# Moving the second branch's sums and splits into the first block-product units, and giving the output tiles other PSUM banks

## The chip, the cores and the metric

The kernel runs on one core of one Trainium2 chip, as one program with one launch. The metric is the device time of that program in microseconds; the kernel before took 1213.66 us (median of 3 runs, 1212.82 to 1214.16). Five engines take part, each with a queue of its own that it works off in order: TensorE (PE, matrix products into PSUM), VectorE (DVE), ScalarE (ACT), GpSimd (POOL) and SyncE (SP, which here only issues DMA transfers). An instruction that waits holds up everything behind it in its engine's queue.

## The reference, cut to what matters

```python
h = rmsnorm(x, mix_norm[l])
proj = h @ w_in[l]                       # q, k, v, su, sv, g_a, g_b
y_att = sliding_window_attention(q, k, v, ...)
y_sgu = chunked_spatial_gating(su, sv, ...)
merged = (jax.nn.sigmoid(g_a) * (y_att @ w_oa[l])
          + jax.nn.sigmoid(g_b) * (y_sgu @ w_ob[l]))
x = x + merged @ w_out[l]
x = x + conv_gated_mlp(rmsnorm(x, ffn_norm[l]), w_up[l], ...)
```

Sequence and model width are both 1024, in float32. The change touches the lines from the gates g_a and g_b to `merged @ w_out`.

## The kernel before, in words

**Exact products in three passes.** A float32 operand is split into a high part (a copy in the PE's reduced format, made by ScalarE through `copy_hi`) and a low part (the operand minus the high part, made by VectorE or GpSimd). A product of two split operands is three matmuls: high by high, high by low, low by high.

**Block products.** The large matrix products use a scheme of seven block products in place of eight (the class `Blocks`). The operands are cut in two by two blocks. A left operand gives A11, A12, A22 and the sums S1 to S4, a right operand gives B11, B21, B22 and the sums T1 to T4. The seven products are A11·B11, S3·T3, A12·B21, S1·T1, A22·T4, S2·T2 and S4·B22. They go into four half tiles of PSUM, g0 and g1 (together the tile `zg`) and v0 and v1 (`zv`). Between them three temporaries have to be kept: x1 (ScalarE's copy of g0 after A11·B11), x7 (ScalarE's copy of v0 after S3·T3, less S1·T1) and u2 (ScalarE's copy of x1 + v1). A12·B21 adds onto g0, so TensorE can't start it until the x1 copy is done; A22·T4 adds onto v0 and waits for the x7 copy.

**The gate stage** (`gates`, with `v_end` and `gate_pair`) computes the pre-activations of both gates, eight pairs of one tile of 128 columns for each gate, 12 matmuls to each of the seven products. `gate_out` takes a finished tile, applies tanh on ScalarE (`th`), and stores it to DRAM from SP's queue. The tile of the b gate is finished by `last_sum` (an addition and a scaling on VectorE) one step late, after the next pair has begun. The last pair, `gate_pair(7, ...)`, has no successor. In its place it issues what the next stage needs: weight loads and splits (`job_load`, `job_split`), and the sums (`y_sum`) and splits (`y_split`) of the right operand of the next stage. There are two right operands: uT for branch b (the spatial gating unit), and ya for branch a (attention), which is read back from DRAM. `y_sum("a", ...)` works in place: T1 goes over B11, T3 over B12, T2 over B22 and T4 over B21 of ya. So a block must be split before the sum that overwrites it. `y_split` is one ScalarE copy of 128x1024 and one subtraction of the same size on the engine named.

**The unit stage** (`branch`, `B_UNITS`) computes the two branch products. Eight units, called u0 to u7 here, each compute two tiles of 128 columns of one branch: 42 matmuls, 6 to each product. In the kernel before the order is b0, a0, b1, a1, b2, a2, b3, a3. A unit is two jobs, `first` (A11·B11, S3·T3, A12·B21, S1·T1) and `second` (A22·T4, S2·T2, S4·B22). `run_jobs` runs job after job: each issues its matmuls up to its `yield`; then the load of the weights four jobs on and the split of those two jobs on are issued, and then the rest of the job. At the end of a b unit the product is multiplied by its gate into a merged tile m (L1311); at the end of an a unit it is multiplied by its gate in place (L1313). `m_add` then adds the a product to m, and splits m for the next product: `copy_hi` on ScalarE, the low parts on GpSimd in four halves that are kept in the list `lo_late` and issued one per job. `m_add` runs late, inside the first job of the following unit; only for the last unit it runs at once, with the low parts on VectorE. The gate tiles come back from DRAM through `th_load`, one unit ahead.

**The output tiles** (`out_tile`) compute merged @ w_out, 48 matmuls for each of the eight tiles. Each takes a PSUM tile from `PS`, which goes round the list `psum["P"]`: two pools, each listed twice and with two tiles of 128x1024, eight banks together. The first two output tiles run over the first six contraction steps, and their last two steps come after that, since those wait for the last pair of m. The last output tile is computed in two halves, each in a PSUM tile of its own.

**What sets the order.** The whole program is written out by hand: the order of calls in the source is the order of instructions on each engine. The units, hooks and jobs are Python closures, so an instruction's place in its engine's queue is where the closure is called.

Of the kernel before, what the change touches and what calls it, by code (L numbers as in the profile page):

```python
# [41 lines left out]
def body(ctx, tc, nc, a):  # L42
# [8 lines left out]
    def nm(s):  # L51
        uid[0] += 1
        return f"{s}_{uid[0]}"
# [17 lines left out]
        return late_by(zr[0], "Z", s, dt, shape, off)  # L71

    def PS(s):
        pools_ = psum["P"]
        pools_.append(pools_.pop(0))
        return pools_[-1].tile([128, 1024], F, tag="P", name=nm(s))
# [628 lines left out]
    def job_split(i):  # L705
        if i < len(jobs):
            job_w[i] = jobs[i][1](job_w[i])
# [3 lines left out]
    def run_jobs():  # L711

        for i in range(len(jobs) - 1):
            m = jobs[i][2](job_w.pop(i))
            next(m)
            if i == 17:
                job_split(18)
                next(m)
            job_load(i + 4)
            if i != 16:  # L720
                job_split(i + 2)
            for _ in m:
                pass
            if lo_late:
                lo_late.pop(0)()


    s3_cm = tc.tile_pool(name="s3p", bufs=1)
# [381 lines left out]
    def gate_pair(c, prev):  # L1110
# [26 lines left out]
        if nx:  # L1137
            nx.sums_q()
            nx.split_p()
            nx.split_s3()  # L1140
        else:
            job_split(0)
            job_load(2)
            y_split("a", "B11", nc.gpsimd)
            y_split("a", "B22", nc.gpsimd)
        q.prod(q.g1, "S1", "T1")
        sub(nc.vector, x7, x7, q.g1)
        if nx:
# [5 lines left out]
        if nx:  # L1154
            nx.split_q()
        else:
            job_split(1)
            y_sum("a", "T1")
            y_sum("a", "T3")
            y_sum("a", "T2")  # L1160
        if c == 5:
            ya_load()
        if c < 6:
# [8 lines left out]
        q.prod(q.g1, "S4", "B22", more=True)  # L1172
        if not nx:
            y_split("b", "B22")
            y_split("a", "B21")
            y_sum("a", "T4")
        return q

    yb = {"b": {}, "a": {}}
# [40 lines left out]
    def gates():  # L1220
        q = v_end()
        for c in range(1, 8):
            q = gate_pair(c, q)
        q.last_sum()
        gate_out(("b", 7), q.zg)
        gates_close()
        th_load(0)
        y_split("a", "T3")
        y_split("a", "T1")
        y_split("a", "T2", nc.gpsimd)  # L1230
        y_split("a", "T4", nc.gpsimd)

    B_UNITS = [(br, j) for j in range(4) for br in "ba"]
    ms = {}

    def th_load(u):
# [32 lines left out]
    un = {"late": None}  # L1269

    def branch(u, part):
        br, j = B_UNITS[u]

        def first(w):
            q = un["q"] = Blocks(w, yb[br], None, 2)
            x1, x7, q.u2 = (s3_pool.tile([128, 512], F, tag=t, name=nm(n)) for n, t in
                            (("x1", "x1"), ("x7", "s3"), ("u2", "s3h")))
            un["x"] = x1, x7
            q.prod(q.g0, "A11", "B11")
            nc.scalar.copy(x1, q.g0)  # L1280
            q.prod(q.v0, "S3", "T3")
            nc.scalar.copy(x7, q.v0)
            q.prod(q.g0, "A12", "B21", more=True)
            q.prod(q.g1, "S1", "T1")
            yield
            sub(nc.vector, x7, x7, q.g1)
            if un["late"]:
                un["late"]()

        def second(w):  # L1290
            q = un["q"]
# [22 lines left out]
            un["late"] = (lambda: m_add(u, j, q)) if br == "a" else None  # L1314
            if u == 7:
                un["late"]()

        jobs.append((lambda: branch_load(u, part), lambda r: branch_split(r, part), (first, second)[part]))

# [2 lines left out]
    def m_add(u, j, q):  # L1322
# [5 lines left out]
        for e, z in enumerate((q.zg, q.zv)):  # L1328
# [1 line left out]
            m, h, l = ms.pop(c), mhi[i][:, c % 4, :], mlo[i][:, c % 4, :]  # L1330
            nc.vector.tensor_tensor(m, m, z, op=ALU.add)
            copy_hi(h, m)
            if u == 7:
                nc.vector.tensor_tensor(l, m, h.bitcast(F), op=ALU.subtract)
            else:
                lo_late.extend(m_lo(m, h, l, x) for x in (L, H))

    def m_lo(m, h, l, x):
        return lambda: nc.gpsimd.tensor_tensor(l[:, x], m[:, x], h[:, x].bitcast(F), op=ALU.subtract)
# [8 lines left out]
    def open_out():  # L1348
# [14 lines left out]
            pools["d" + n] = [dr.tile([128, 512], F, tag=f"{n}_{i}", name=f"{n}_{i}") for i in range(HK)]  # L1363
        for i in (0, 1):
            out_load(D_ORDER[i])
        psum["P"].insert(0, psum["P"].pop())

    D_ORDER = (0, 4, 1, 5, 2, 6, 3, 7)
    HK = NPAIR // 2
# [636 lines left out]
```

## Time and profile before

| | |
|---|---|
| median of 3 runs | 1213.66 us |
| the profiled execution | 1212.38 us |
| its span | 1210.7 us |
| TensorE busy | 1172.4 us, 97% |
| VectorE busy | 869.9 us, 72% |
| GpSimd busy | 637.0 us, 53% |
| ScalarE busy | 566.4 us, 47% |
| gate pair 7 on TensorE | 360.4 to 379.5 us |
| units u0 to u7 on TensorE | 379.5 to about 477 us |
| output tiles on TensorE | 482.9 to 572.8 us |

How to read the rows that follow in the prediction. A row of the waits view says which engine and line waited for which engine, tile and line: microseconds in total, times, longest. A row of the windows view gives a stretch and its length, then for each engine the busy time and in brackets the number of instructions, then the granted clock of TensorE as a share of full speed, the busy share of the DMA engines and GB/s. A row of the timeline gives the start and the duration in microseconds, the engine, the line, the operation, the tile written and the tiles read, the shapes, a count where instructions were merged and, in square brackets, the idle time before it and what ended that. A row of one tile's view gives the shortest, median and longest duration in ns, then the start of the first and the last. A row of the DMA view gives a transfer's count, its size and the median time to landing. L1213 is the subtraction in `y_split`; L620 is the helper `sub`, used for sums and differences at many places; L87 is `copy_hi`.

### The profile page before, as it was taken

The numbers are of one execution on the slowest core, as the hardware profiler recorded it, in microseconds if no ns is written. First come the engines' busy times: TensorE is split into PE (matmuls) and PEld (weight loads), VectorE is DVE, ScalarE is ACT, GpSimd is POOL, SyncE is SP. The second block draws the span as 40 slices with busy tenths as digits, with TensorE's granted clock in tenths as the row PEclk, the third lists the DMA queues.
The fourth block names the chain that finished last, engine by engine and source line by source line (L and its number), as shares of the span: only waits on it lengthen the run. The fifth ranks groups of instructions, "written<-read, shape, count | busy, mean of one in ns | idle before, by whom it ended". The sixth has DMA issues, their size and how long they took to land.

```text
span 1210.7 us, 15917 instructions
## 1 busy us (share of the span) xinstructions
PE 1172.4 (97%) x5842; PEld 992.1 (82%) x5842; DVE 869.9 (72%) x1032; ACT 566.4 (47%) x878; POOL 637.0 (53%) x442
## 2 busy tenths in 40 slices
PE   8999999999996798999999999999999999999998
PEld 8999989888885686888888888888888888888887
DVE  7789966732347576387887888878887888775674
ACT  8555567643435454133544444444544445434331
POOL 2467684598674467234776767767677642000000
PEclk9999999999998899999999999999999999999999
DMA  7010145254653566054554555556554448975471
GB/s 276 27 54 19 53 148 209 89 145 128 194 150 113 183 205 212 36 183 121 165 141 133 171 130 157 130 135 164 137 165 122 114 168 277 382 259 191 140 232 72
DMA packets 79934, 185.51 MB, mean 153 GB/s; under 512 B 9072, under 2 KB 16496, under 8 KB 79728
## 3 DMA queue, kind: packets, MB, share of 16 engines
q1 hardware_dynamic: 72144, 164.57, 39.8%
q0 software_dynamic: 7456, 15.73, 8.2%
q10 hardware_dynamic: 256, 4.19, 1.0%
q8 instruction: 46, 0.75, 0.3%
q14 instruction: 32, 0.26, 0.1%
HBM read 145.40 MB, written 47.45 MB: 159 GB/s over the span
## 4 chain that ended last, share of the span: by engine, by line
PE 62%; POOL 1%; ACT 1%; DVE 1%; issue 1%; DMA 0%; POOLq 0%; ACTq 0%
PE pz L1058 38%; PE pd L1820 10%; PE pdy L1820 7%; PE px L91 2%; PE px L93 2%; PE px L92 2%; DMA lq<-wup 0%; POOL pl L1017 0%; POOL lr L620 0%; ACT T L87 0%; ACT y L87 0%; DVE res L1840 0%; DVE pz L1313 0%; POOL ql L1017 0%; DVE pz L620 0%
## 5 line engine op out<-in xcount | busy, mean ns | idle before, releaser
L1058 PE MATMUL pz<-T,qh 128*128 128x512 f32 x472 | 145.6, 390 | 0.0
L1058 PE MATMUL pz<-B,ph 128*128 128x512 f32 x352 | 109.6, 392 | 0.3 <-ACT x L1660 0.3
L1058 PEld LDWEIGHTS pz<-T,qh 128*128 128x128 f32 x472 | 88.4, 188 | 18.7 <-ACT u L883 0.3
L1017 POOL TENSOR_TENSOR pl<-lp,ph 128x1024 fp32r<-128x1024 f32 x30 | 73.1, 2437 | 53.1 <-ACT ph L87 53.1
L1058 PE MATMUL pz<-T,ql 128*128 128x512 f32 x236 | 91.8, 389 | 0.0
L1058 PE MATMUL pz<-y,wjh 128*128 128x512 f32 x224 | 70.4, 396 | 19.2 <-ACT x L1280 19.2
L1017 POOL TENSOR_TENSOR ql<-lq,qh 128x1024 fp32r<-128x1024 f32 x30 | 76.7, 2557 | 9.1 <-ACT qh L87 9.1
L1058 PEld LDWEIGHTS pz<-B,ph 128*128 128x128 f32 x352 | 65.1, 188 | 16.2 <-ACT x L1660 3.2
L1074 DVE TENSOR_TENSOR pz<-pz,rstd_b 128x1024 f32<-128x1024 f32 x60 | 73.9, 1232 | 4.6 <-ACT rstd_b L141 2.5
L1058 PE MATMUL pz<-T,s3h 128*128 128x512 f32 x232 | 71.4, 389 | 0.0
L1058 PE MATMUL pz<-B,pl 128*128 128x512 f32 x176 | 68.6, 390 | 0.0
L1820 PE MATMUL pd<-bh,ah 128*128 128x512 f32 x176 | 68.5, 389 | 0.0
L1820 PE MATMUL pd<-bl,ah 128*128 128x512 f32 x176 | 68.5, 389 | 0.0
L1820 PE MATMUL pd<-bh,al 128*128 128x512 f32 x176 | 68.5, 389 | 0.0
L1058 PEld LDWEIGHTS pz<-y,wjh 128*128 128x128 f32 x224 | 42.9, 192 | 28.5 <-ACT x L1280 19.6
L1058 PE MATMUL pz<-T,AX 128*128 128x512 f32 x264 | 63.4, 389 | 0.0
L1058 PE MATMUL pz<-B,AX 128*128 128x512 f32 x264 | 63.4, 389 | 0.0
L620 DVE TENSOR_TENSOR x<-x,pz 128x512 f32<-128x512 f32 x36 | 24.5, 681 | 51.7 <-PE pz L1058 43.9
L1017 POOL TENSOR_TENSOR s3l<-lq,s3h 128x512 fp32r<-128x512 f32 x20 | 25.9, 1297 | 61.9 <-ACT s3h L87 61.9
L1058 PEld LDWEIGHTS pz<-T,AX 128*128 128x128 f32 x264 | 49.6, 188 | 10.3
L1058 PEld LDWEIGHTS pz<-B,AX 128*128 128x128 f32 x264 | 49.6, 188 | 10.3
L1515 DVE SCALAR_TENSOR_TENSOR tv<-pz,cp,tv 128x1023 f32<-128x1023 f32 (+1 forms) x44 | 56.2, 1278 | 0.8
(353 smaller groups left out, 3596.1 us busy)
## 6 DMA issues: line engine op xcount, KB each, us to landing
lp<-wup SPq DMA_DIRECT2D x22, 512.0 KB, 3.8
lq<-wup SPq DMA_DIRECT2D x22, 512.0 KB, 4.2
ra<-wdown SPq DMA_DIRECT2D x44, 256.0 KB, 4.8
b<-T SPq DMA_DIRECT2D x44, 256.0 KB, 3.6
lq<-wup POOLq DMA_DIRECT2D x42, 256.0 KB, 5.4
B<-tv SPq DMA_DIRECT2D x33, 256.0 KB, 2.0
T<-tt SPq DMA_DIRECT2D x33, 256.0 KB, 2.1
b<-B SPq DMA_DIRECT2D x33, 256.0 KB, 3.4
```

The source lines that it names most:

```text
L91: nc.tensor.matmul(out, wh, mh, start=first, stop=False, **kw)
L92: nc.tensor.matmul(out, wh, ml, start=False, stop=False, **kw)
L93: nc.tensor.matmul(out, wl, mh, start=False, stop=last, **kw)
L620: eng.tensor_tensor(out, x, y, op=op)
L1017: nc.gpsimd.tensor_tensor(l, r, h.bitcast(F), op=ALU.subtract)
L1058: nc.tensor.matmul(o, p[:, k, :], m, start=not more and k == 0 and j == 0, stop=k == nk - 1 and j == 2, skip_group_check=True)
L1074: nc.vector.tensor_tensor(z, z, rstd_b, op=ALU.mult)
L1515: nc.vector.scalar_tensor_tensor(t[:, j:], p[:, 0:1024 - j], cw[:, ci, 2 - j:3 - j], t[:, j:], op0=ALU.mult, op1=ALU.add)
L1820: nc.tensor.matmul(o[d], p[:, k - k0, m], q[:, k - k0, :], start=new and k == 0 and j == 0, stop=k == HK - 1 and j == 2, skip_group_check= ...
```

## The change

The sums and splits of branch a's operand leave `gate_pair(7)` and the end of `gates`, and are called from hooks inside the units: the splits of B11, B22 and B21 at the end of u0's first job (all on VectorE now), the four sums and the splits of T3 and T1 at the end of u0's second job, and the splits of T4 (VectorE) and T2 (GpSimd) at the end of u1's first job. Branch a's first unit comes third in the new order, b0, b1, a0, b2, a1, b3, a2, a3. The last gate's sum, its tanh, its store, the closing of the gate stage's pools and the first `th_load` move from the end of `gates` to a place behind u0's first four products, so behind u0's x1 and x7 copies on ScalarE. In `m_add`, the low part of the first tile of each pair is made at once on VectorE, between the two additions; of the second tile one half is made at once on GpSimd and one is kept in `lo_late`, which is emptied ahead of the rest of a job. The nine PSUM tiles of the output stage are taken by an explicit list.

```diff
     def PS(s):
+        if psum.get("next"):
+            return psum["next"].pop(0).tile([128, 1024], F, tag="P", name=nm(s))
         pools_ = psum["P"]
...
             if i != 16:
                 job_split(i + 2)
+            if lo_late:
+                lo_late.pop(0)()
             for _ in m:
                 pass
-            if lo_late:
-                lo_late.pop(0)()
...
             job_split(0)
             job_load(2)
-            y_split("a", "B11", nc.gpsimd)
-            y_split("a", "B22", nc.gpsimd)
...
             job_split(1)
-            y_sum("a", "T1")
-            y_sum("a", "T3")
-            y_sum("a", "T2")
...
             y_split("b", "B22")
-            y_split("a", "B21")
-            y_sum("a", "T4")
...
             q = gate_pair(c, q)
+        un["hooks"]["end"] = lambda: gates_end(q)
+        un["hooks"][0, 0] = lambda: [y_split("a", n) for n in ("B11", "B22", "B21")]
+        un["hooks"][0, 1] = a_begin
+        un["hooks"][1, 0] = a_end
+
+    def gates_end(q):
         q.last_sum()
         gate_out(("b", 7), q.zg)
         gates_close()
         th_load(0)
+
+    def a_begin():
+        for n in ("T1", "T3", "T2", "T4"):
+            y_sum("a", n)
         y_split("a", "T3")
         y_split("a", "T1")
+
+    def a_end():
+        y_split("a", "T4")
         y_split("a", "T2", nc.gpsimd)
-        y_split("a", "T4", nc.gpsimd)
-
-    B_UNITS = [(br, j) for j in range(4) for br in "ba"]
+
+    B_UNITS = [("b", 0), ("b", 1), ("a", 0), ("b", 2), ("a", 1), ("b", 3), ("a", 2), ("a", 3)]
...
             q.prod(q.g0, "A12", "B21", more=True)
             q.prod(q.g1, "S1", "T1")
+            if u == 0:
+                un["hooks"]["end"]()
             yield
             sub(nc.vector, x7, x7, q.g1)
             if un["late"]:
                 un["late"]()
+            un["hooks"].get((u, 0), lambda: None)()
...
             if u == 7:
                 un["late"]()
+            un["hooks"].get((u, 1), lambda: None)()
...
             copy_hi(h, m)
-            if u == 7:
+            if u == 7 or e == 0:
                 nc.vector.tensor_tensor(l, m, h.bitcast(F), op=ALU.subtract)
             else:
-                lo_late.extend(m_lo(m, h, l, x) for x in (L, H))
+                m_lo(m, h, l, L)()
+                lo_late.append(m_lo(m, h, l, H))
...
-        psum["P"].insert(0, psum["P"].pop())
+        psum["next"] = [psum["P"][i] for i in (0, 1, 2, 3, 0, 2, 1, 3, 2)]
```

More of the change, by code (lines that the diff above doesn't have):

```diff
@@ L1267, in branch_split @@
         return {n: (h[:, 2 * i:2 * i + 2], l[:, 2 * i:2 * i + 2]) for i, n in enumerate(B_PARTS[part])}
-    un = {"late": None}
+    un = {"late": None, "hooks": {}}
     def branch(u, part):
```

## The prediction

> **What bounds the kernel now.** I read the page, then the waits of TensorE, then windows around its two long waits, then each engine's timeline there.
>
> ```profile
> PE 1172.4 (97%) x5842; PEld 992.1 (82%) x5842; DVE 869.9 (72%) x1032; ACT 566.4 (47%) x878; POOL 637.0 (53%) x442
> ...
> PE pz L1058 <- ACT x L1280: 19.2, 1, 19.2
> PE px L91 <- DVE m L1331: 5.8, 1, 5.8
> ...
> 401.50:405.50 4.00, 3.97 (x10) 3.15 (x11) 0.00 (x0) 0.46 (x1) 3.60 (x2) 0.51 0.97 311
> 405.50:476.00 70.50, 70.50 (x312) 58.36 (x311) 47.58 (x57) 33.34 (x56) 46.36 (x39) 1.00 0.60 195
> ...
> 483.00:488.00 5.00, 5.00 (x14) 3.94 (x15) 3.04 (x3) 1.86 (x2) 0.00 (x0) 0.57 0.15 58
> ```
>
> TensorE is busy for 97% of the span, so a change can win only idle time or half-speed time. The idle time is nearly all in two waits: 19.2 us for the x1 copy of the first block-product unit (called u0; the next is u1, and so on to u7), and 5.8 us ahead of the first output tile. In the undisturbed window 312 products take 70.5 us, 0.226 us each. A unit has 42 of them, 9.5 us. After each wait the granted clock is about half: 10 products in 4.0 us lose 4.0 - 2.26 = 1.7 us, 14 in 5.0 us lose 5.0 - 3.16 = 1.8 us. The two places cost 19.2 + 1.7 + 5.8 + 1.8 = 28.5 us, and that is the most this change can win.
>
> Where do the 19.2 us come from? These rows are the end of the gate stage on TensorE, VectorE and ScalarE:
>
> ```profile
> 374.02 2.88 PE L1058 MATMUL pz<-T,gax 128*128 128x512 f32 x12
> 381.96 0.39 PE L1058 MATMUL pz<-y,wjl 128*128 128x512 f32 x1
> ...
> 372.37 5.75 POOL L1213 TENSOR_TENSOR y<-ya,y 128x1024 fp32r<-128x1024 f32 x2
> 372.64 3.22 DVE L1213 TENSOR_TENSOR y<-uT,y 128x1024 fp32r<-128x1024 f32 x1 [0.45 <-ACT y L87]
> 375.79 3.41 DVE L1213 TENSOR_TENSOR y<-yt,y 128x1024 fp32r<-128x1024 f32 x1
> 379.12 3.99 DVE L620 TENSOR_TENSOR ya<-ya 128x1024 f32<-128x1024 f32 x2
> 384.37 0.69 DVE L1067 TENSOR_TENSOR pz<-x,pz 128x512 f32<-128x512 f32 x1
> 386.49 0.70 DVE L620 TENSOR_TENSOR pz<-x,pz 128x512 f32<-128x512 f32 x1
> 387.22 1.23 DVE L1074 TENSOR_TENSOR pz<-pz,rstd_b 128x1024 f32<-128x1024 f32 x1
> 390.36 1.05 ACT L87 ACTIVATE y<-ya 128x1024 fp32r<-128x1024 f32 x1
> 394.16 0.69 DVE L1077 TENSOR_TENSOR pz<-u,pz 128x512 f32<-128x512 f32 x1
> 394.88 1.23 DVE L1074 TENSOR_TENSOR pz<-pz,rstd_b 128x1024 f32<-128x1024 f32 x1
> 396.20 1.02 ACT L1087 ACTIVATE th<-pz 128x1024 f32<-128x1024 f32 x1 [4.79 <-issue]
> 397.12 3.88 ACT L87 ACTIVATE y<-ya 128x1024 fp32r<-128x1024 f32 x4
> 398.20 2.36 DVE L1213 TENSOR_TENSOR y<-ya,y 128x1024 fp32r<-128x1024 f32 x2 [2.08 <-ACT y L87]
> 400.90 0.57 ACT L1280 COPY x<-pz 128x512 f32<-128x512 f32 x1
> ```
>
> TensorE has done u0's first two products at 382.2 (the product at 381.96 plus 0.226). The copy that it needs runs at 400.90, because ScalarE works in order: ahead of it stand the last gate's tanh at 396.20, which waits for VectorE's backlog, and four split copies (3.88 us). L1067 could have run when its product ended (374.02 + 2.88 = 376.9). It ran at 384.37, behind two splits stretched to 3.22 and 3.41 us while GpSimd ran its own two, and two sums of ya.
>
> **The change part by part.**
>
> Gate 7 is relieved. Two splits of the second branch's y leave GpSimd, one split (aB21) and four sums leave VectorE, and the four split copies leave ScalarE's queue ahead of x1. L1067 then starts at 376.9. Add 0.69 for it, 0.57 for ScalarE's copy, twice 0.70 and 1.23 for the scale: 380.9 with handovers. VectorE goes on with three low parts of 1.18 each (2.36 for two). The tanh (1.02) and the split copy of bB22 (1.05) bring ScalarE to 383.0, and the x1 copy ends at 383.6. TensorE waits **1.4 us** in u0 instead of 19.2.
>
> The removed work is not gone, and most of it now stands ahead of u1's x1 copy. This is the term that decides. The hook at the end of u0 puts the sums T1, T3, T2, T4 on VectorE, and the split copies of T3 and T1 on ScalarE ahead of u1's x1 copy. The chain, step by step, with durations from the rows above and from these:
>
> ```profile
> 406.19 1.15 ACT L87 ACTIVATE wjh<-wj 128x512 fp32r<-128x512 f32 x2 [4.23 <-issue]
> 418.64 0.69 DVE L1298 TENSOR_TENSOR pz<-x,pz 128x512 f32<-128x512 f32 x1 [1.96 <-PE pz L1058]
> 422.10 2.36 DVE L1313 SCALAR_TENSOR_TENSOR pz<-th,pz 128x1024 f32<-128x1024 f32 x2
> ...
> th<-dth SPq DMA_DIRECT2D x16, 512.0 KB, 5.1
> ```
>
> - VectorE ends gate 7's three low parts at 380.9 + 3.5 = 384.4, and the last sum and scale (394.16 to 396.11, 1.95) at 386.3. The tanh ends at 387.4.
> - ScalarE: u1's two weight copies (1.15) to 388.5, the copy of aB11 (1.05) to 389.6. VectorE's low parts of aB11, aB22 and aB21: 3.5, to 393.1. GpSimd makes u1's weight parts at the same time, so I add 0.4: 393.5.
> - u0's own combination, L1298 up to the last sum, takes 422.10 - 418.64 = 3.4, to 396.9. The two products with the gate take 2.35, to 399.3.
> - The sums T1 and T3 (of the low parts' size, two of 1.18) end at 401.7, their copies (two of 0.97 by the four in 3.88) at 403.6, and x1 (0.57) at 404.2.
>
> TensorE resumes in u0 at 383.6, needs 30 products for the rest of it (6.8, to 390.4) and 12 for u1's first two (2.7, to 393.1). It waits 404.2 - 393.1 = **11.1 us** in u1. Half speed follows, as after both long waits of before: **1.7 us**. In the later steps of this part (T4 and T2 of the second branch, for u2) VectorE and GpSimd have a unit's length more, so I cost them at nothing; without that cover it is 0.4 us.
>
> Moved with the gate's end on SP's queue: the last tanh's store and the two loads of th for u0, still between the third and the fourth weight load. They are issued at 388 to 389; by the median of 5.1 us they land at about 394, ahead of L1311 at 396.9. Cost nothing; what lands later than 396.9 adds to the 11.1 us for each us, since VectorE's sums queue behind L1311.
>
> The low part of one merged tile in each pair goes from GpSimd to VectorE, between that pair's two additions:
>
> ```profile
> 426.11 2.34 DVE L1331 TENSOR_TENSOR m<-m,pz 128x1024 f32<-128x1024 f32 x2
> 430.93 0.59 ACT L1280 COPY x<-pz 128x512 f32<-128x512 f32 x1
> 432.24 0.59 ACT L1282 COPY x<-pz 128x512 f32<-128x512 f32 x1 [0.72 <-PE pz L1058]
> ...
> 481.49 1.21 DVE L1331 TENSOR_TENSOR m<-m,pz 128x1024 f32<-128x1024 f32 x1
> 483.83 1.23 DVE L1334 TENSOR_TENSOR ml<-m,mh 128x1024 fp32r<-128x1024 f32 x1 [1.12 <-ACT mh L87]
> 484.97 1.21 DVE L1331 TENSOR_TENSOR m<-m,pz 128x1024 f32<-128x1024 f32 x1
> ```
>
> The last pair already has this form: its second addition starts 3.48 us after the first (it waits for ScalarE's copy, then runs the low part), against 1.13 where the two follow each other. L1298 comes 2.35 us later in the unit that carries the additions, and the next unit's x1 copy with it. That copy ends at 431.5, and TensorE wants it at 432.2 (the x7 copy waits for its product there), a margin of 0.7. It happens in u3 and u5, paid in u4 and u6: 2 x 1.7 = **3.4 us**. Bounds: nothing, if ScalarE takes the copy earlier, and 2 x 2.35 = 4.7.
>
> ```profile
> 505.24 2.39 POOL L108 TENSOR_TENSOR wjl<-wj,wjh 128x1024 fp32r<-128x1024 f32 x1 [23.51 <-ACT wjh L87]
> 505.60 3.12 DVE L1423 SCALAR_TENSOR_TENSOR h<-ac,cp,rstd_b 128x1024 f32<-128x1024 f32 x1
> 522.38 1.29 DVE L1423 SCALAR_TENSOR_TENSOR h<-ac,cp,rstd_b 128x1024 f32<-128x1024 f32 x1
> ```
>
> A VectorE operation of 1.29 us took 3.12 when it started 0.4 after a GpSimd one: it ended 1.1 after that one's end. So GpSimd's work can hold up these low parts; above I took 0.4 for it, its bounds are 0 and 1.0 in u1's chain. The Trainium skill (SBUF — State Buffer, section "SBUF: two separate sides") says the pair of ports is locked for a whole instruction, which speaks against moving subtractions with two SBUF operands to VectorE. By that rule alone, with a full wait in u1's chain and at each of the pair additions, the sum below would be some 3 us worse.
>
> The banks. The first output tile now takes u6's bank, free since u7 began, so the 5.8 us and the 1.8 us behind them go. What is late next: the fifth contraction step's upper half, whose low part is still on GpSimd, behind the second output tile's weights (2.39). By that order it ends about **0.8 us** after TensorE wants it. The last tile's second half now takes the bank of the sixth tile, whose last reader is this:
>
> ```profile
> 562.65 1.21 DVE L1443 TENSOR_TENSOR sq<-sq,px 128x1024 f32<-128x1024 f32 x1
> ...
> L93 PE MATMUL px<-mh,wjl x128: 389/389/632, 483.8 to 572.4; 128*128 128x512 f32 x128
> ```
>
> The half has 24 products (5.4 us) and the last of all ends at about 572.6, so it starts at 567.2, 3.3 us after that reader: nothing.
>
> **The sum.** Before: 28.5. After: 1.4 + 11.1 + 1.7 + 3.4 + 0.8 = 18.4. The gain is 10.1 us. The profiled execution took 1212.38 us (its span is 1210.7); it becomes 1202.3. The median of the runs is 1213.66, 1.28 above it, so the forecast is **1203.6**.
>
> **The rivals.**
>
> *The backlog costs less* (1197.4). The chain to u1's x1 is 2 us shorter, with copies overlapping (a 1.05 us copy lets the next start after 0.95), and the 3.4 and 0.8 are hidden. After: 1.4 + 9.1 + 1.7 = 12.2, a gain of 16.3. For it: the margins of 0.7 and 0.8 are small numbers read off one execution. Against it: the chain is in order on two engines, and few of its handovers can shrink.
>
> *Half speed after each short wait* (1208.7). Three waits of 1.4 to 1.7 us then cost 1.7 more each, 5.1. For it, from the start of the kernel:
>
> ```profile
> PE pkv L91 <- ACT x L87: 1.9, 1, 1.9
> ...
> 6.30:9.40 3.10, 3.08 (x14) 3.06 (x15) 1.99 (x5) 2.56 (x6) 0.00 (x0) 1.00 1.00 399
> 9.50:11.10 1.60, 1.56 (x14) 1.36 (x12) 1.60 (x4) 1.60 (x4) 0.00 (x0) 1.00 1.01 416
> ```
>
> After a wait of 1.9 us 14 products took 3.1 us, and the next 14 took 1.6. Against it: TensorE had only just begun there, and may not have been at full speed before the wait. The Trainium skill (TensorE: Matmul & The Clock Gate, Part 1) halves the clock only after an idle window of about 3.4 us; by that the three are free.
>
> *The wait moves whole* (1212.1, no change). GpSimd's work stretches the second branch's sums and splits as it stretched the old ones: 3.22 + 3.41 + 3.99 against four of 1.18 is 5.9 us, here in u1, and 1.3 (2.39 less the 1.1 by which VectorE ended after GpSimd) at each of two additions: 8.5 less gain. For it: the same operations. Against it: in u1's chain GpSimd has only two weight parts, not two whole splits besides.
>
> *VectorE falls behind in every unit* (1220.6, slower). A unit with a pair addition needs VectorE for 0.69 + 3.48 + 1.21 + 3.46 + 2.36 = 11.2 us, more than its 9.5; the other for 0.69 + 3.46 + 2.36 = 6.5. If the second doesn't make good what the first loses, six units wait 1.7 us each, with half speed after each: 1.4 + 11.1 + 1.7 + 6 x 3.4 + 0.8 = 35.4, 6.9 more than 28.5. It decides where two units need more than 19.0 us; the rows give 17.7, and every GpSimd wait adds to that.
>
> **How the numbers follow.** Forecast 0.55, cheaper backlog 0.13, half speed 0.15, wait moves whole 0.08, falls behind 0.09. About 0.2% is what the spread of the runs (1212.82 to 1214.16) lets one tell from no change. Faster: 0.55 + 0.13 + 0.15 = 0.83; within 0.2%: 0.08; slower: 0.09. The range goes from just under the first rival, 1197.0, to half speed plus u1's upper bounds (0.6 for GpSimd, 1.2 for th or the later units): 1210.5.
>
> **What would show it.** The waits of TensorE for the x1 copy (L1280 of before) are one of 1 to 2 us and one of about 11, then two of under 2; the wait on the pair addition ahead of the first output tile is gone, with full clock there. In the timeline, two split copies of ya stand directly ahead of u1's x1 copy. I am wrong if u1's wait is under 8 or over 14 us, if short waits are followed by slow products, or if an output tile waits for a bank.

## The result, and the profile after

| | before | after |
|---|---|---|
| median | 1213.39 us (4 runs, 1212.82 to 1214.16) | 1202.68 us (4 runs, 1201.76 to 1203.1) |
| ratio to before, 95% interval | | 0.991 [0.9893, 0.9927] |
| span of the profiled execution | 1210.7 us | 1201.4 us |

The medians are 10.7 us apart, the spans 9.3; the profiled execution of the changed kernel is the slowest of its four (1203.1 us). The changed kernel has new line numbers: the x1 copy is L1287 (L1280 before), the matmuls of the block products L1060 (L1058), `y_split` L1208 (L1213), the pair addition L1342 (L1331), `sub` L622 (L620), `copy_hi` L89 (L87).

The engines' row of the page and the x1 row of the waits, for the changed kernel:

```profile
PE 1173.8 (98%) x5842; PEld 991.5 (83%) x5842; DVE 873.2 (73%) x1038; ACT 565.6 (47%) x878; POOL 620.0 (52%) x433
```

```profile
PE pz L1060 <- ACT x L1287: 14.8, 4, 11.1
```

The one wait of 19.2 us for the x1 copy has become four waits of 14.8 us together, and the 5.8 us ahead of the first output tile are gone. The timeline around the first two units shows two of the four, and what is late for the longest; the other two, of 1.2 us each, are the x1 waits of u4 and u6 (they end at 438.02 and 458.90). These are rows of TensorE, VectorE, ScalarE and GpSimd:

```profile
383.78 0.73 PE L1060 MATMUL pz<-y,wjh 128*128 128x512 f32 x2 [1.23 <-ACT x L1287]
404.76 1.22 PE L1060 MATMUL pz<-y,wjh 128*128 128x512 f32 x2 [11.15 <-ACT x L1287]
410.82 0.40 PE L1060 MATMUL pz<-y,wjl 128*128 128x512 f32 x1
...
377.15 0.70 DVE L1069 TENSOR_TENSOR pz<-x,pz 128x512 f32<-128x512 f32 x1 [2.31 <-PE pz L1060]
384.56 0.69 DVE L1079 TENSOR_TENSOR pz<-u,pz 128x512 f32<-128x512 f32 x1
389.59 4.48 DVE L1208 TENSOR_TENSOR y<-ya,y 128x1024 fp32r<-128x1024 f32 x3 [1.95 <-ACT y L89]
394.00 0.68 DVE L1308 TENSOR_TENSOR pz<-x,pz 128x512 f32<-128x512 f32 x1
397.46 2.35 DVE L1321 SCALAR_TENSOR_TENSOR m<-th,pz 128x1024 f32<-128x1024 f32 x2
399.73 2.48 DVE L622 TENSOR_TENSOR ya<-ya 128x1024 f32<-128x1024 f32 x2
...
386.55 1.03 ACT L1089 ACTIVATE th<-pz 128x1024 f32<-128x1024 f32 x1 [2.33 <-DVE pz L1076]
402.24 2.00 ACT L89 ACTIVATE y<-ya 128x1024 fp32r<-128x1024 f32 x2 [6.11 <-DVE ya L622]
404.15 0.56 ACT L1287 COPY x<-pz 128x512 f32<-128x512 f32 x1
...
388.17 2.55 POOL L1273 TENSOR_TENSOR wjl<-wj,wjh 128x512 fp32r<-128x512 f32 x2 [11.22 <-ACT wjh L89]
```

Read ScalarE's rows from below. The x1 copy of u1 runs at 404.15, straight behind two split copies of ya. Those were free to run only when VectorE had made the sums T1 and T3 (399.73 + 2.48 = 402.2), and the sums stood behind u0's products with the gate, u0's combination from L1308 on, and three low parts. ScalarE itself was idle for 6.11 us ahead of the two copies, with nothing to do but what it could not start.

The windows of the changed kernel (same columns as before; the granted clock is the third number from the right) show the price behind the long wait, and the handover to the output tiles:

```profile
376.00:392.00 16.00, 14.77 (x65) 11.88 (x65) 11.65 (x12) 10.34 (x13) 3.50 (x4) 1.00 0.31 103
405.00:410.00 5.00, 5.00 (x12) 3.89 (x13) 2.00 (x2) 0.29 (x2) 0.00 (x0) 0.50 0.03 14
475.00:490.00 15.00, 14.86 (x66) 11.97 (x65) 11.69 (x12) 4.61 (x5) 4.94 (x3) 1.00 0.43 140
```

The view of the output tiles (durations in ns, then the start of the first and the last), and two rows of TensorE's timeline in their sixth contraction step:

```profile
L93 PE MATMUL px<-mh,wjh x128: 388/389/398, 475.4 to 562.7; 128*128 128x512 f32 x128
```

```profile
482.84 0.39 PE L93 MATMUL px<-mh,wjh 128*128 128x512 f32 x1
483.37 0.50 PE L94 MATMUL px<-ml,wjh 128*128 128x512 f32 x1
```

u0, with its wait of 1.23 us, ran at full clock. After the 11.15 us in u1 it was 0.50: 14 products start between 404.76 and 410.82, in 6.06 us where 14 x 0.226 = 3.16 would do, so 2.9 us are lost. The output tiles begin at 475.4 at full clock; before, they began at 482.9. In their sixth contraction step (the 35th product; the prediction calls it the fifth) a product of the low part of m starts 0.53 us behind its neighbour, 0.3 more than usual.

So the gain has two parts of very different size. Up to the first output product, the units' own loss went from 19.2 + 1.7 to 14.8 and about 3 of half speed. These rows leave out the slips just beside the waits; counted from the start of one product to the start of the next, with 0.227 us as the normal step, the units lose 21.3 us before and 19.3 after, so only 2 us of the gain lie there. The larger part, the wait for the bank and the slow products behind it, came at the handover to the output tiles.

### The profile page after: what moved, and what is told of

Read it like the earlier page. It is cut to its first block, busy times and chain, and to the rows that moved or that the text cites. A ratio compares the mean times of both kernels' runs of the same rounds, so it can differ in the third digit from the quotient of the medians.

```text
span 1201.4 us, 15911 instructions
## 1 busy us (share of the span) xinstructions
PE 1173.8 (98%) x5842; PEld 991.5 (83%) x5842; DVE 873.2 (73%) x1038; ACT 565.6 (47%) x878; POOL 620.0 (52%) x433
## 4 chain that ended last, share of the span: by engine, by line
PE 59%; DVE 0%; POOL 0%; issue 0%; POOLq 0%
PE pz L1060 35%; PE pd L1832 10%; PE pdy L1832 8%; PE px L95 2%; PE px L94 2%; PE px L93 2%; DVE res L1852 0%; PE pz L140 0%; PE pz L1503 0%; POOL ml L1351 0%; POOL wjl L110 0%; POOLq L110 0%
## 5 line engine op out<-in xcount | busy, mean ns | idle before, releaser
L1060 PE MATMUL pz<-T,qh 128*128 128x512 f32 x472 | 145.6, 390 | 0.0
L1060 PE MATMUL pz<-B,ph 128*128 128x512 f32 x352 | 109.6, 393 | 0.0
L1060 PEld LDWEIGHTS pz<-T,qh 128*128 128x128 f32 x472 | 88.5, 188 | 18.7 <-ACT u L885 0.3
L1060 PE MATMUL pz<-T,ql 128*128 128x512 f32 x236 | 91.8, 389 | 0.0
L1060 PE MATMUL pz<-y,wjh 128*128 128x512 f32 x224 | 71.9, 403 | 14.9 <-ACT x L1287 14.8
L1060 PEld LDWEIGHTS pz<-B,ph 128*128 128x128 f32 x352 | 65.1, 188 | 15.8 <-ACT x L1672 2.8
L1060 PE MATMUL pz<-T,s3h 128*128 128x512 f32 x232 | 71.4, 389 | 0.0
L1060 PE MATMUL pz<-B,pl 128*128 128x512 f32 x176 | 68.6, 390 | 0.0
L1060 PEld LDWEIGHTS pz<-y,wjh 128*128 128x128 f32 x224 | 42.9, 194 | 26.4 <-ACT x L1287 16.5
L1060 PE MATMUL pz<-T,AX 128*128 128x512 f32 x264 | 63.4, 389 | 0.0
L1060 PE MATMUL pz<-B,AX 128*128 128x512 f32 x264 | 63.4, 389 | 0.0
L1273 POOL TENSOR_TENSOR wjl<-wj,wjh 128x512 fp32r<-128x512 f32 (+1 forms) x32 | 36.8, 1170 | 49.2 <-ACT wjh L89 49.2
L622 DVE TENSOR_TENSOR x<-x,pz 128x512 f32<-128x512 f32 x36 | 24.5, 681 | 46.8 <-PE pz L1060 46.8
L1060 PEld LDWEIGHTS pz<-T,AX 128*128 128x128 f32 x264 | 49.6, 188 | 10.3
L1060 PEld LDWEIGHTS pz<-B,AX 128*128 128x128 f32 x264 | 49.6, 188 | 10.3
```

The costliest lines, as they stand in the source:

```text
L622: eng.tensor_tensor(out, x, y, op=op)
L1060: nc.tensor.matmul(o, p[:, k, :], m, start=not more and k == 0 and j == 0, stop=k == nk - 1 and j == 2, skip_group_check=True)
```

## Experiments

All ratios are to the kernel before on the same chip, with the 95% interval.

**The banks alone.** The kernel before, with only the list of PSUM tiles.

```diff
-        psum["P"].insert(0, psum["P"].pop())
+        psum["next"] = [psum["P"][i] for i in (0, 1, 2, 3, 0, 2, 1, 3, 2)]
```

> The kernel before with the explicit list of PSUM tiles for the output stage, and nothing else of the change. My theory: the banks work by themselves. The wait of 5.8 us ahead of the first output tile and the slow products behind it (11 products at 0.43 us in place of 0.23, 2.1 us) go, the 19.2 us in u0 stay: 1213.4 - 7.9 = 1205.5 us. Rival: the bank was not the only thing that held the first output tile; the split of the merged tiles on GpSimd ends last there in the old order, a wait of 3 us or more takes the place of the old one, and the time stays above 1208.

Measured: 1205.99 us, ratio 0.9934 [0.9919, 0.9949]. The waits keep the 19.2 us for x1, and there is no row of `px` waiting for a pair addition any more (the rival's wait on GpSimd's split did not come):

```profile
PE pz L1060 <- ACT x L1282: 19.2, 1, 19.2
```

The bank list alone gives some 8 us of the change's 10.7.

**Everything but the banks.** The changed kernel with the old rule for the PSUM tiles.

```diff
-        psum["next"] = [psum["P"][i] for i in (0, 1, 2, 3, 0, 2, 1, 3, 2)]
+        psum["P"].insert(0, psum["P"].pop())
```

> The changed kernel with the old rule for the output stage's PSUM tiles. My theory: the units by themselves win 1.5 us up to the first output tile (u0 and u1 wait 1.2 and 11.2 us where it was 19.2, with 1.2 us more of half speed, and u4 and u6 wait 1.8 each). With the old banks the first output tile waits again for the last pair's addition, which comes 2.35 us later than before because the low part of the pair ahead now stands between two additions: a wait of about 8.1 us and 2.1 to 2.9 us of half speed, so 1202.7 + 10 to 11 = 1213 us, no gain at all. Rival: the two parts add up, 1202.7 + 7.9 = 1210.6 us, with a wait of 5.8 us there.

Measured: 1214.19 us, ratio 0.9998 [0.9989, 1.0008]: all the moving of sums and splits wins nothing by itself. Its wait ahead of the output tiles, then TensorE's and VectorE's timeline there:

```profile
PE px L93 <- DVE m L1342: 8.8, 1, 8.8
```

```profile
484.19 0.77 PE L93 MATMUL px<-mh,wjh 128*128 128x512 f32 x1 [8.84 <-DVE m L1342]
...
471.99 1.21 DVE L1342 TENSOR_TENSOR m<-m,pz 128x1024 f32<-128x1024 f32 x1
474.32 1.44 DVE L1345 TENSOR_TENSOR ml<-m,mh 128x1024 fp32r<-128x1024 f32 x1 [1.13 <-ACT mh L89]
475.69 1.21 DVE L1342 TENSOR_TENSOR m<-m,pz 128x1024 f32<-128x1024 f32 x1
476.82 0.68 DVE L1308 TENSOR_TENSOR pz<-x,pz 128x512 f32<-128x512 f32 x1
482.82 1.22 DVE L1342 TENSOR_TENSOR m<-m,pz 128x1024 f32<-128x1024 f32 x1
```

The wait grew from 5.8 to 8.8 us. With the old rule the first output tile needs the bank that the first addition of u7's own pair reads. TensorE came to the place 1.7 us sooner than before (484.19 - 8.84 = 475.35, against 482.9 - 5.8), and that addition came 1.3 later (482.82, against 481.49): the new order ends in two units of branch a, so u6's pair, with its low part in between, falls into u7 (471.99 to 476.90) ahead of u7's own combination. What the units win, this wait takes back. With the new banks it falls away together with its growth. So the two parts of the change do not add: 8 alone and 0 alone make 10.7 together.

**The old order of units.** The changed kernel with b0, a0, b1, a1 and so on.

```diff
-    B_UNITS = [("b", 0), ("b", 1), ("a", 0), ("b", 2), ("a", 1), ("b", 3), ("a", 2), ("a", 3)]
+    B_UNITS = [(br, j) for j in range(4) for br in "ba"]
```

> The changed kernel with the units in the old order b0, a0, b1, a1, b2, a2, b3, a3. My theory: the second branch's operand is then wanted one unit earlier, while VectorE still makes it. u1 (a0) waits about 1.3 us for B11's split, 12 to 13 us for T3's, 4 to 5 us for T4's, and the pair additions cost 1.8 us in three units, not two: some 11 us more than the changed kernel, about 1214 us. Rival: the order of the units matters little, since VectorE and ScalarE do the same work in the same order: within 3 us of the changed kernel.

Measured: 1212.63 us, ratio 0.999 [0.9981, 0.9999]. TensorE's waits:

```profile
PE pz L1060 <- ACT y L89: 12.1, 2, 10.1
PE pz L1060 <- ACT x L1287: 4.9, 4, 1.2
PE pz L1060 <- DVE y L1208: 4.2, 3, 1.8
```

Beside the four short waits for x1, it is the operand itself that is late here: the second unit needs T3 of branch a (`y`) before its split exists. Putting b1 ahead of a0 is what gives the moved work a unit's time. This run has the new banks, so the old order costs as much as the banks win.

**The split copies behind u1's x1 and x7.** The splits of T3 and T1 are called in the middle of u1's first job, so ScalarE's queue has the x1 copy first.

```diff
+    def a_mid():
         y_split("a", "T3")
         y_split("a", "T1")
...
+        un["hooks"][1, "mid"] = a_mid
...
+            un["hooks"].get((u, "mid"), lambda: None)()
             yield
```

> The changed kernel, only the splits of T3 and T1 of the second branch called behind u1's x1 and x7 copies in place of the end of u0; the four sums stay where they are. My theory: u1's wait of 11.15 us is set by ScalarE's order, the two split copies that wait for VectorE's sums. x1 then follows u2's weight copies at 396.1 and TensorE resumes at 396.7: a wait of about 3.5 us, a new one of about 2.8 us at u1's S4*B22 (it adds onto g1, which VectorE reads behind its backlog), half speed after the first or not: some 5 us less, 1197.7 us. Rival: VectorE's backlog itself holds x1 (its buffer, or u0's combination), and moving ScalarE's copies wins under 1.5 us: above 1201.

Measured: 1200.92 us, ratio 0.9893 [0.9876, 0.9909], span 1198.6, which is 2.8 under the changed kernel's. TensorE's waits, two windows behind the two long ones, and VectorE's timeline:

```profile
PE pz L1060 <- ACT x L1290: 6.7, 4, 3.0
PE pz L1060 <- DVE x L622: 3.6, 1, 3.6
```

```profile
397.00:403.00 6.00, 6.00 (x15) 4.71 (x16) 5.83 (x6) 1.15 (x2) 1.08 (x2) 0.52 0.85 264
409.00:413.00 4.00, 4.00 (x11) 3.14 (x12) 3.26 (x4) 1.42 (x3) 4.00 (x3) 0.58 0.31 98
```

```profile
404.84 3.43 DVE L1208 TENSOR_TENSOR y<-ya,y 128x1024 fp32r<-128x1024 f32 x2
408.20 0.68 DVE L622 TENSOR_TENSOR x<-x,pz 128x512 f32<-128x512 f32 x1
```

The longest wait for x1 fell from 11.15 to 3.0 us: ScalarE's order was its cause. But u1 then waited 3.6 us at S4·B22, which writes the half tile that VectorE's subtraction L622 (x7 less S1·T1) reads; VectorE came to it at 408.20, behind the sums and two low parts. And half speed came twice, 15 products in 6.0 us and 11 in 4.0. Two waits of some 3 us cost more clock here (6.0 - 3.4 and 4.0 - 2.5, 4.1 us) than one of 11, so only 2.8 of the 5 us expected came, and 1.8 by the medians. The median lies at the edge of the rival's 1201, and the ratio's interval overlaps the changed kernel's: it is the trace that decides, not the time.

**The pair's first low part on GpSimd.**

```diff
-            if u == 7 or e == 0:
+            if u == 7:
                 nc.vector.tensor_tensor(l, m, h.bitcast(F), op=ALU.subtract)
+            elif e == 0:
+                m_lo(m, h, l, L)()
+                m_lo(m, h, l, H)()
```

> The changed kernel, only the low part of the first tile of each pair made by GpSimd in two halves at once, in place of VectorE between the two additions. My theory: the waits in u4 and u6 (1.2 us each in the records, 1.8 us each with what stands around them) come from VectorE's second addition, which follows 2.35 us later; they go, and no other wait comes: 1202.7 - 3.6 = 1199.1 us. Rival: GpSimd becomes the late one, the first output tile waits for low parts, and the time is within 1 us of 1202.7.

Measured: 1200.0 us, ratio 0.9883 [0.9868, 0.9898], span 1198.1. The waits for x1:

```profile
PE pz L1060 <- ACT x L1287: 12.4, 2, 11.2
```

Two of the four waits are gone, those in u4 and u6, and the span is 3.3 us shorter, the median 2.7 (the ratio's interval still touches the changed kernel's). Some 0.6 us of it is not this part's doing: behind the same wait in u1 this execution has 11 products in 4.77 us at half speed, where the changed kernel's has 14 in 6.06. So this part of the change is a loss of about 3 us, and there is a simple way round it.

**Is the half speed due to TensorE's idling?** The first attempt put 42 more matmuls (A11·B11 into g1, overwritten later) behind S3·T3 in u1.

> The changed kernel with 42 more matmuls (9.5 us at 0.226) in u1 between S3*T3 and A12*B21, into g1, which S1*T1 overwrites later; they do no useful work. My theory: the wait of 11.2 us in u1 is for ScalarE's x1 copy and TensorE's own work doesn't lengthen it, so the 42 fit in; the remaining wait is about 1.7 us, the products behind it run at full speed, and the 2.9 us of half speed go: 2.9 us less than the changed kernel, 1199.8 us. Rival: the slow products are not the idle time's doing (the operands or the new bank make them slow), they stay slow, and the time is that of the changed kernel within 0.5 us.

Measured: 1213.04 us, ratio 0.9988 [0.9979, 0.9998]. By TensorE's timeline the first of the added products stood still too:

```profile
405.60 1.22 PE L1060 MATMUL pz<-y,wjh 128*128 128x512 f32 x2 [11.12 <-ACT x L1287]
```

They write g1, the other half of the PSUM tile whose half g0 the x1 copy reads, and they were issued behind that copy; they waited for it as A12·B21 does. So they ran after the wait, not in it, and cost what they take: 42 x 0.226 = 9.5 us, and the span is 9.6 us longer than the changed kernel's. The question stayed open. The second attempt issues eight such products ahead of the x1 copy in the program:

```diff
             q.prod(q.g0, "A11", "B11")
+            if u == 1:
+                for _ in range(8):
+                    q.prod(q.g1, "A11", "B11")
             nc.scalar.copy(x1, q.g0)
```

> The changed kernel, where the second unit also computes A11·B11 eight more times (48 matmuls, 10.9 us at 0.227 us each) into its second product bank, right after the first A11·B11 and ahead of x1's copy; the results are overwritten, the output stays the same. TensorE so works through nearly all of the 11.1 us that it waits for x1 in the changed kernel, and ScalarE's copy of x1 still comes when it came (404.15 us), since it is behind two split copies there and not behind TensorE. Theory (products run at half speed after this wait because TensorE was idle): wait for x1 under 1 us, no products of 0.43 us behind it, and the 2.9 us of half speed are won: about 1199.8 us by the median of the changed kernel, 1202.7. Rival (half speed has another cause that this stretch brings, such as the transfers or ScalarE's and VectorE's reads): the products behind the copy still take 0.43 us for about 6 us, and the time stays at 1202.7 us.

Measured: 1201.62 us, ratio 0.9897 [0.9884, 0.9911], span 1199.8. ScalarE's and TensorE's timeline, and the window behind the wait:

```profile
404.97 0.56 ACT L1290 COPY x<-pz 128x512 f32<-128x512 f32 x1
405.59 0.73 PE L1060 MATMUL pz<-y,wjh 128*128 128x512 f32 x2 [0.26 <-ACT x L1290]
```

```profile
408.00:413.00 5.00, 5.00 (x24) 4.14 (x23) 3.09 (x3) 3.05 (x4) 3.83 (x3) 1.00 0.03 11
```

The copy still ends at 405.5, for ScalarE's reasons; TensorE waits 0.26 us, and behind it 24 products run in 5.0 us at full clock where the changed kernel ran 12. The rival (the stretch itself is slow, whatever TensorE did before) falls. The mean granted clock is 1.000 in three of the four executions; in the fourth, the slowest (1202.95 us), it is 0.997, and where its slow stretch lay is not on record. 48 useless matmuls made the kernel no slower, and by the spans 1.6 us faster. The intervals of the two ratios overlap, so it is the clock in the profile that settles the cause, not the time. Of the 2.9 us expected, 0.8 us is an offset that this execution had already at u0 (its x1 wait ends at 384.60, against 383.78); where the remaining 0.5 went wasn't followed.

**Spreading the second branch's preparation.** This variant and the next three keep the low part on GpSimd and place each sum and split where its engine has room. The diffs show the placements alone; that the old hooks go and `y_sum` takes an engine is left out. The first one:

```diff
             job_split(1)
+            y_split("a", "B22", nc.gpsimd)
+            y_split("a", "B11", nc.gpsimd)
...
             y_split("b", "B22")
+            y_sum("a", "T1", nc.gpsimd)
+            y_split("a", "B21", nc.gpsimd)
...
+        un["hooks"][0, 0] = lambda: (y_sum("a", "T3"), y_sum("a", "T2"), y_split("a", "T3", nc.gpsimd),)
+        un["hooks"][0, 1] = lambda: (y_sum("a", "T4", nc.gpsimd),)
+        un["hooks"][1, 0] = lambda: (y_split("a", "T4"), y_split("a", "T1", nc.gpsimd), y_split("a", "T2", nc.gpsimd),)
```

> The changed kernel with the low parts as in the run with the low parts on GpSimd, and the second branch's work spread: splits of B22 and B11 on GpSimd in gate 7 behind the split of the second weights, the sum T1 and the split of B21 on GpSimd at gate 7's end, the sums T3 and T2 on VectorE and the split of T3 on GpSimd at the end of u0's first job, the sum T4 on GpSimd at the end of u0's second job, the splits of T4 (VectorE), T1 and T2 (GpSimd) at the end of u1's first job. My theory: u1's wait is VectorE's and ScalarE's chain of three splits, u0's combination, the gate products and four sums; GpSimd stood idle from 377 to 388 and 398 to 410, and with that work there no wait over 2.5 us is left between u0 and u2, so no half speed either. The units then lose some 3 us in place of 19.3: about 1187 us. Rival: GpSimd and VectorE hold each other up, as in the kernel before (two splits of 3.2 and 3.4 us in place of 1.2), waits of 5 us or more with half speed come back, and the time is 1193 or more.

Measured: 1191.79 us, ratio 0.9817 [0.9802, 0.9832], span 1190.3: about 11 us under the changed kernel. What is left of u1's wait is 1.03 us. In u0 it is now 2.17, and this wait is followed by half speed (timeline, then the window):

```profile
384.91 1.22 PE L1060 MATMUL pz<-y,wjh 128*128 128x512 f32 x2 [2.17 <-ACT x L1281]
383.34 1.04 ACT L89 ACTIVATE y<-ya 128x1024 fp32r<-128x1024 f32 x1
384.28 0.57 ACT L1281 COPY x<-pz 128x512 f32<-128x512 f32 x1
```

```profile
385.00:388.50 3.50, 3.50 (x9) 2.77 (x10) 3.50 (x2) 0.34 (x1) 3.49 (x2) 0.55 0.00 0
```

One split copy of 1.04 us ahead of x1 on ScalarE, B21's, makes 1.23 into 2.17, and nine products in 3.5 us lose 1.5 more. The 1187 us expected, with no half speed, was missed for that reason among others.

A second placement, with B22 and T3 moved instead:

```diff
-            y_split("a", "B21", nc.gpsimd)
+            y_sum("a", "T3", nc.gpsimd)
+            y_split("a", "B22", nc.gpsimd)
...
+        un["hooks"][0, 0] = lambda: (y_split("a", "T1", nc.gpsimd), y_sum("a", "T2"), y_split("a", "B21"), y_split("a", "T3", nc.gpsimd),)
+        un["hooks"][1, "mid"] = lambda: (y_split("a", "T2"), y_sum("a", "T4", nc.gpsimd),)
+        un["hooks"][1, 0] = lambda: (y_split("a", "T4", nc.gpsimd),)
```

> As the run before, spread otherwise: the split of B11 on GpSimd in gate 7 behind the split of the second weights; the sums T1 and T3 and the split of B22 on GpSimd at gate 7's end; at the end of u0's first job the split of T1 (GpSimd), the sum T2 and the split of B21 (VectorE), the split of T3 (GpSimd); behind u1's x1 and x7 copies the split of T2 (VectorE) and the sum T4 (GpSimd); at the end of u1's first job the split of T4 (GpSimd). My theory: about the same, 1187 us, with a little more GpSimd work ahead of u1, so that a wait of 0.5 to 1 us may stand at u1's A12*B21. Rival: as for the run before, 1193 or more.

Measured: 1193.32 us, ratio 0.9827 [0.9812, 0.9842]: waits of 2.2 and 2.3 us for x1 in u0 and in u1, each with 3.4 us at a granted clock of 0.50 behind it. That is the rival's time, 1193, but not its cause: no wait of 5 us or more came back.

Two more have no copy of branch a directly ahead of u0's x1, and make T3's sum on GpSimd and T2's on VectorE between the halves of u0. The first of them, against the first placement; the other differs from it as its expectation says:

```diff
-            y_split("a", "B21", nc.gpsimd)
...
+        un["hooks"][0, "mid"] = lambda: (y_sum("a", "T3", nc.gpsimd), y_sum("a", "T2"),)
+        un["hooks"][0, 0] = lambda: (y_split("a", "T2", nc.gpsimd), y_split("a", "B21", nc.gpsimd),)
+        un["hooks"][0, 1] = lambda: (y_sum("a", "T4"),)
+        un["hooks"][1, "mid"] = lambda: (y_split("a", "T1", nc.gpsimd),)
+        un["hooks"][1, 0] = lambda: (y_split("a", "T3"), y_split("a", "T4", nc.gpsimd),)
```

> The changed kernel with the low parts of the first unit of each pair on GpSimd and with the second branch's preparation spread: copies of B22 and B11 in gate pair 7 with their subtractions on GpSimd, T1's sum on GpSimd behind that pair, T3's sum on GpSimd and T2's on VectorE between the first unit's halves, then the splits of T2 and B21 with GpSimd subtractions, T4's sum at the end of the first unit, T1's split in the middle of the second, T3's and T4's behind it. No copy of the second branch is ahead of the first unit's x1 and x7 on ScalarE. Theory (e7_spread_a lost its 2.2 us in the first unit and the 1.3 us of half speed behind it to one such copy of 1.0 us): the first unit's wait falls to about 1.2 us and half speed there goes: about 1189.5 us. Rival (GpSimd's work of 3.3 us beside VectorE's stretches the last gate's multiplication and so the tanh and the copies behind it): at least 1191.8 us, e7_spread_a's time.

> As e10_spread_c, with B21's split (subtraction on GpSimd) first behind the first unit's middle, T3's split there too, T2's split with its subtraction on VectorE at the end of the first unit, and T4's sum behind the second unit's middle. Theory: as e10_spread_c, about 1189.5 us, with a wait of 1.2 us in the first unit. Rival: a product of the third unit waits for T2 or T4, which here are made last, and the time is 1191 us or more.

Measured: 1192.37 us, ratio 0.982 [0.9807, 0.9834], and 1192.92 us, ratio 0.9828 [0.9814, 0.9841]: no better than the first placement. The timeline of the former (TensorE, GpSimd, VectorE), and two of its windows:

```profile
384.61 0.72 PE L1060 MATMUL pz<-y,wjh 128*128 128x512 f32 x2 [1.24 <-ACT x L1282]
393.89 0.72 PE L1060 MATMUL pz<-y,wjh 128*128 128x512 f32 x2 [3.53 <-DVE x L622]
408.57 0.50 PE L1060 MATMUL pz<-y,wjl 128*128 128x512 f32 x1 [1.43 <-POOL wjl L1268]
...
382.60 6.56 POOL L622 TENSOR_TENSOR ya<-ya 128x1024 f32<-128x1024 f32 x2
383.52 3.39 DVE L1211 TENSOR_TENSOR y<-yt,y 128x1024 fp32r<-128x1024 f32 x1
386.83 3.41 DVE L1211 TENSOR_TENSOR y<-uT,y 128x1024 fp32r<-128x1024 f32 x1
393.16 0.68 DVE L622 TENSOR_TENSOR x<-x,pz 128x512 f32<-128x512 f32 x1
```

```profile
394.50:399.00 4.50, 4.50 (x14) 3.55 (x13) 1.99 (x3) 3.33 (x6) 4.50 (x4) 0.62 1.01 342
408.50:411.50 3.00, 2.93 (x13) 2.39 (x14) 2.72 (x4) 1.89 (x5) 3.00 (x3) 1.00 0.84 330
```

The theory held for u0's x1: 1.24 us, and no slow products behind it. The rival named the loss, though not its place. GpSimd's two sums run beside two of VectorE's low parts, which take 3.39 and 3.41 us instead of 1.22. VectorE's subtraction L622 comes 4.4 us later for it, and S4·B22 waits for that. The other one has the same wait, 3.5 us. Its rival (T2 or T4 late in the third unit) did not come about; its time came out above 1191 by another way. No placement tried here is free of both losses.

## Why the prediction was right

The sum was made against the profiled execution: 28.5 us of loss before, 18.4 after. The trace of after, term by term:

| term | forecast | measured |
|---|---|---|
| u0's wait for x1 | 1.4 | 1.2 |
| u1's wait for x1 | 11.1 | 11.15 |
| half speed behind it | 1.7 | 2.9 |
| u4 and u6 | 3.4 | 3.7 (by the starts of products) |
| first output tile | 0.8 | 0.3 |
| sum | 18.4 | 19.3 |

28.5 - 19.3 = 9.2, and the spans differ by 9.3. (By the starts of products throughout, from u0 to the last output product, TensorE loses 29.9 us before and 20.5 after, 9.4 less.) So the sum was 0.9 us too hopeful: it forecast 1202.3 us for the profiled execution, which took 1203.1. That the median came out below the forecast (1202.7 against 1203.6) is luck of the executions: the 1.28 us that the forecast adds for the median did not return, since this time the profiled execution was the slowest.

- **Gate 7.** L1067 (now L1069) was to start at 376.9; it starts at 377.15. The x1 copy was to let TensorE go on at 383.6; it goes on at 383.78.
- **The chain in u1.** Each step came 0.2 to 0.6 us late, and TensorE reached its wait some 0.4 late too, so the difference held; that it held to 0.1 us is errors that cancelled. The tanh was forecast to end at 387.4 and ended at 387.6; the sums T1 and T3 at 401.7, measured 402.2; x1 at 404.2, measured 404.7. Within the chain one term was too small: the three low parts took 4.48 us, not 3.5 + 0.4, beside GpSimd's two weight parts (388.17 to 390.72). That is the upper bound named for it, 1.0. The run with the split copies behind x1 shows that ScalarE's order was the cause, as argued.
- **Half speed** was the term mis-sized. The forecast carried over the 1.7 us of before. It lasted 6 us here and cost 2.9. The price is not fixed by the wait: behind the same wait of 11.1 us the run with the low part on GpSimd lost 2.3 us (11 products in 4.77 us), the first filled one 2.1 (10 in 4.40) and the one with the old banks 1.9 (9 in 3.90). Counted in this way, by the starts of products, the kernel before lost 1.9 too (9 in 3.96). So 1.7 was just under the low end of what this wait cost, and the changed kernel's profiled execution drew the high end. That it is due to TensorE's idling was only assumed, and the filled wait shows it.
- **The low part between the pair's additions.** It was forecast at 1.7 in each of u4 and u6. Their waits are 1.2 (14.8 less 1.23 and 11.15, halved), but by the starts of products u4 loses 1.9 us and u6 1.8: a wait row leaves out the slips beside it, a small one 1.7 us ahead of each wait among them. The run with this part on GpSimd has neither loss.
- **The banks** were as forecast, and so was what is late next: the late product starts at 483.37, when GpSimd's low part ends behind the weights (482.02 and 1.29, to 483.31). What the prediction did not see is that the old rule would have grown with the new order to 8.8 us, so that the moved work shows its gain only together with the new banks.
- **The gate's DMAs.** VectorE goes straight on from the combination to L1321 at 397.46 with no idle time before it: the gate tiles had landed, and the cost of nothing was right.

The rivals fell as follows. Half speed behind each short wait did not happen: u0's window stands at clock 1.00. (The row given for that rival, of the kernel's start, has its slow products at a granted clock of 1.00, so by itself it was no sign of a halved clock.) The wait did not move whole, and VectorE did not fall behind in every unit: there are four waits, not seven. The backlog was not cheaper by 2 us.

## What to carry to other kernels

Work that is moved out of one wait usually stands in front of another queue's next deadline; here the question was which copies stand ahead of x1 on an in-order ScalarE, and that one chain, written out with durations from the trace, gave the new wait to 0.1 us, though single steps were up to 0.6 off. Cost the parts of a change together as well as apart: the bank list was worth 8 us alone, the rest nothing alone, and the rest some 3 us once the banks were free. A subtraction on GpSimd is no free cover for one on VectorE beside it, and a wait that is shortened only to 2 or 3 us may keep its price in clock. One execution does not give that price: the same wait cost between 1.9 and 2.9 us.

## What the runs showed of the hardware

- **A wait of 2.2 us already brings half speed; one of 1.4 did not.** Behind waits of 0.26, 1.23 and 1.43 us the clock stayed at 1.00. Behind 2.17 us nine products took 3.5 us (0.55), the waits of 2.18 and 2.30 us in the second placement each had 3.4 us at 0.50 behind them, behind 3.0 fifteen took 6.0 (0.52), behind 11.15 twelve took 5.0 (0.50). The Trainium skill (TensorE: Matmul & The Clock Gate, Part 1) puts it at an idle window of about 3.4 us whose phase runs free of the work. That the short waits are free agrees; the 2.17 us here does not fit a whole idle window.
- **The halved clock comes in pieces of about 3.4 us, on a grid of its own.** The windows view puts 0.50 at 384.9 to 405.4 (20.5 us) and 480.5 to 487.3 (6.8) in the kernel before, 397.0 to 410.7 (13.7) in the changed kernel, 396.0 to 409.7 (13.7) with the low part on GpSimd, 399.7 to 409.9 (10.2) in the first filled run and 384.8 to 388.2 (3.4) in the first placement. These lengths are 6, 2, 4, 4, 3 and 1 times 3.41 us, and the two beginnings in the kernel before lie 28 times 3.41 apart. It begins inside a long wait, and behind the 3.53 us wait of the third placement only at 395.0, so that the first products there, from 393.89, still run at full rate (0.72 us for two). What a wait costs depends on where its end falls in such a stretch:

```profile
397.10:410.60 13.50, 5.83 (x14) 4.58 (x15) 9.94 (x10) 3.65 (x6) 0.75 (x2) 0.50 0.51 158
396.10:409.60 13.50, 4.63 (x11) 3.67 (x12) 10.86 (x11) 3.19 (x5) 1.95 (x2) 0.50 0.56 185
```

The first row is the changed kernel's, the second that of the run with the low part on GpSimd: the waits end at 404.76 and 404.96, and 14 and 11 products fall into what is left. A window with a phase of its own, as the Trainium skill (TensorE: Matmul & The Clock Gate, Part 1) has it, would look so; that it is the reason wasn't tried.
- **GpSimd beside VectorE.** A subtraction with two operands in SBUF took 3.4 us on VectorE instead of 1.22 when GpSimd's sum of the same kind had started first (two of them in 6.56 us); it ended 1.1 us behind the first of them. The Trainium skill (SBUF — State Buffer, section "SBUF: two separate sides") describes this as an exclusive lock for a whole instruction; the rows agree.
- **In this program a PSUM tile is one thing to the waits.** Products into g1 waited 11.12 us for a copy that read g0, the other half of the same tile.
